# Retention queries and keys as block products, attention-value products in another order, bias rows made once

## The chip, the cores and the metric

The kernel runs on one core of one Trainium2 chip. The metric is the device time of one execution in microseconds (us), lower is better. The core has a matrix engine (PE; PEld is its weight loading), a vector engine (DVE), an activation engine (ACT), GpSimd (POOL) and a queue-only engine (SP), which run side by side and wait for one another through semaphores. Each engine works through its instructions in program order. SP, ACT and POOL issue DMAs; only POOL issues those that add to their destination.

## The reference, cut to what matters

Two layers (DEPTH 2) over 512 tokens of width 1024, float32. Each layer projects the input x to many columns at once and then mixes:

```python
z = einsum('bsd,dc->bsc', x, w_in) + b_in
q_a, k_a, v_a, q_r, k_r, v_r, g_r, gate_a, gate_b = split(z)
# attention: 18 heads of 64 in three groups (window, dilation)
# retention: 4 heads; q, k 256 wide, v and gate 512 wide
t1, t2 = t[..., :128], t[..., 128:]                 # rot(), for q and for k
rot = concatenate([t1 * cos - t2 * sin, t1 * sin + t2 * cos])
sc = (q . k) * decay_mask;  o = sc . v (+ state);   y_r = group_norm(o)
y_b = silu(g_r) * y_r
merged = sigmoid(gate_a) * (y_a @ w_attn_proj) + sigmoid(gate_b) * (y_b @ w_ret_proj)
x = layer_norm(ALPHA * x + merged @ w_out)
x = layer_norm(ALPHA * x + (silu(x @ w_gate) * (x @ w_up)) @ w_down)
```

What concerns the change is the first line: the columns of the attention values (v_a, 1152), of the retention queries and keys (q_r, k_r, 256 per head each) and of the retention values and gates (v_r, g_r, 512 per head each), with their biases, and the rotation of q_r and k_r.

## The kernel before

**Products.** Every float32 factor is split into a high part and a low part (`hilo`, L91: ACT casts the high part at L92, DVE subtracts it at L93), and every product is three matmuls of 128 rows (`mm3`, L80): high by high, high by low, low by high. All of them stand as L81 in the profile, since the helper `mm` holds the call. Weights come from memory into eight buffers (`raw`, 1024 float32 a partition) by SP, and their parts go into four buffers each of `whi` and `wlo`.

Three schemes make the projections:

- `wstat` (weights stationary, 512 tokens moving): 24 matmuls of 512 columns for 128 output columns. The queries and keys of all retention heads are made so: four `wstat`, 96 matmuls per head.
- `wide` (weights stationary, block scheme): two matrices of 256 output columns share seven block products instead of eight, on halves of the tokens and of the inner dimension. Each block product is 24 matmuls of 256 columns, 168 in all for 2 x 256 output columns. The merge gates and the FFN use it.
- `tall` (tokens stationary, weights moving): the same seven block products for 2 x n columns, each of 24 matmuls of n columns. The attention values use it (n = 288, two calls per layer, t = 0 and 1, called VA below), and the retention values and gates (n = 512, one call per head, called vg(0) to vg(3)).

The operands of the seven products come from class `Right`: four blocks B11, B21, B22 and (inside P1 and P3) B12 of the weights, and the sums P1 = B11 + B12, P3 = B12 + B22, P2 = P1 + B22, P4 = P2 + B21. P1 and P3 are made in memory traffic: SP loads one block (L109), and POOL issues a DMA that adds the other to it (L316). P2 and P4 are DVE additions in P1's buffer (L342). `operands` runs one product ahead: while PE works at one product, ACT (L325) and DVE (L331) make the parts of the next. For `tall` a product has two buffers (two units), for `wide` one.

The order of the products is a table. `ORDER`, which `tall` uses, is 1, 2, 5, 3, 6, 7, 4, with the operands B11, B21, P1, B22, P2, P3, P4. `WIDE` is 1, 5, 6, 2, 7, 3, 4, with the operands B11, P1, P2, B21, P3, B22, P4. Several products add up in one PSUM tile (`CHAIN`): 1, 6, 7, 4 in chain A, 5 and 3 in chain C, 2 alone. What has to leave the chain between two products is copied by ACT to a tile `sn` (L453), and DVE adds or subtracts (L460, L463).

**Order of the work.** The program is written by hand, engine by engine. One list, `side`, holds small pieces of other work (attention, scores and outputs of retention), and `tick` takes from it at the rate that `pace` sets, after each group of three matmuls. In `ret_outputs` of the head before, which runs beside `rotary(h)`, each of four pieces `one(i)` does matmuls (`px<-vr,pj`), statistics on DVE (L855 to L859), a power on POOL (L124) and three tiny DVE steps that wait for it (L125 to L127); `turn(i)` transposes the result.

**Around the change.** A layer begins with attention queries and keys, then VA for t = 0 and 1, then attention, then rotary(0) and vg(0), and for h = 1, 2, 3: rotary(h), vg(h). Each `tall` call is preceded by `bias_rows` (L429): POOL clears a `raw` buffer and loads the two biases into rows 0 and 32 by four small DMAs, DVE and ACT turn them into high and low parts in the one tile `bh`, and a matmul with `ones` as stationary operand (rows 0 and 32 are 1) puts the bias into PSUM. That is done 12 times, 4 for VA and 8 for the heads. In `rotary` (L645) DVE takes each of the four `wstat` results times cos and times sin, the bias added in the same step (L655), subtracts and adds (L659, L660), and `hilo` makes the parts, tile name `rot`.

The names in rows: `raw` a weight buffer, `whi` and `wlo` its parts, `xh`, `xl` the parts of the tokens, `xs` those of the sums of tokens, `ps` and `px` PSUM tiles, `rp` the rotated pieces, `rb` and `bh` the bias rows, `pj` the scores, `vr` the retention values.

Of the kernel before, what the change touches and what calls it, by code (L numbers as in the profile page):

```python
# [18 lines left out]
P = 128  # L19
# [34 lines left out]
def hybrid_kernel(ctx, tc, x, rel_bias, w_in, b_in, w_attn_proj, w_ret_proj, w_out,  # L54
# [40 lines left out]
    def raw(name="raw"):  # L95
        return rawp.tile([P, 1024], F32, tag="raw", name=name)
# [201 lines left out]
    WIDE = tuple(ORDER[i] for i in (0, 2, 4, 1, 5, 3, 6))  # L298
    WIDE1 = tuple(ORDER[i] for i in (0, 1, 2, 4, 3, 5, 6))
# [54 lines left out]
    def pair_right(w1, w2, c, order=WIDE):  # L354
# [17 lines left out]
    def tall(right, n, left, ev, bias_=None):  # L372


        ps = {}
        for (i, an, bn), units in zip(ORDER, right.operands()):
            ks = [(u, k) for u in units for k in range(u[0].shape[1])]
            c = CHAIN[i]
            for a in range(2):
                fresh = i in FIRST  # L380
                if fresh:
                    ps[c, a] = psum("ps")[:, :n]
                if bias_ is not None and i in (1, 5):
# [12 lines left out]
                if i == 6:  # L396
                    ev(3, a, ps["C", a])
            yield

    def wide(right, left, ev):  # L400
# [26 lines left out]

        return Right(src, [(k, n) for k in nk])

    def bias_rows(b1, b2):  # L430

        n = b1.shape[0]
        r = raw("rb")[:, :2 * n]
        pool.memset(r, 0.0)
        for q in (0, BK):
            pool.dma_start(r[q:q + 1, :n], b1.unsqueeze(0))
            pool.dma_start(r[q:q + 1, n:], b2.unsqueeze(0))
        dve.tensor_tensor(out=r[:, n:], in0=r[:, n:], in1=r[:, :n], op=ALU.add)
        h = bh[:, :2 * n]
        act.copy(out=h, in_=r)  # L440
        e = slice(BK, BK + 1)
        dve.tensor_tensor(out=h[e], in0=r[e], in1=h[e].bitcast(F32), op=ALU.subtract)
        return h

    def biased(right, n, rows_, left, right_done):
# [19 lines left out]
        return tall(right, n, x_left, ev, rows_)  # L465
# [158 lines left out]
    def layer(ly, cp):  # L624
# [16 lines left out]
        def slot(name="op", dt=F32R):  # L641
            return opp.tile([P, 2, S], dt, tag="op", name=name)

        def rotary(h):

            rot = []
            for c0 in (C_QR + h * RQ, C_KR + h * RQ):
                us = pair_units(w_l, c0)
                prod = []
                for t in range(2):  # L650
                    ps = wstat(us, t)
                    pr = []
                    for tb in (cos, sin):
                        m = work("rp")
                        dve.scalar_tensor_tensor(out=m, in0=ps, scalar=bcol(c0 + t * P), in1=tb, op0=ALU.add, op1=ALU.mult)  # L655
                        pr.append(m)
# [4 lines left out]
                pair = []
                for src in (t1c, t1s):
                    o_ = slot("rot")
                    hilo(src, o_[:, 0], o_[:, 1])
                    pair.append(o_)
                rot.append(pair)
            heads[h]["q"], heads[h]["k"] = rot

        def ret_values_gates(h):
            cv, cg = C_VR + h * RV, C_GR + h * RV  # L670
# [16 lines left out]
            rows_ = bias_rows(b_l[cv:cv + RV], b_l[cg:cg + RV])  # L687
            yield from biased(halves(w_l, 0, (2, 2), cv, cg, RV), RV, rows_, left, gate)

        with stage("attn") as ap_, stage("attw", 4) as aw:  # L690
            qk = {}
# [16 lines left out]
            if ly == 0:  # L708
# [28 lines left out]
                o32 = work("o32")
                dve.memset(o32[:, :P], 0.0)
                dve.memset(o32[0:1, :P], 1.0)
                dve.memset(o32[BK:BK + 1, :P], 1.0)  # L740
                act.copy(out=ones, in_=o32[:, :P])
# [16 lines left out]
            for t in range(2):  # L758
                c1, c2 = C_VA + t * VB, C_VA + (2 + t) * VB

                def put(i, s, c):
                    nc.sync.dma_start(v_d[i * P:(i + 1) * P, c - C_VA:c - C_VA + VB], s)

                def left(i, ps, s, c1=c1):
                    if s is None:
                        s = work("sn")[:, :VB]
                        act.copy(out=s, in_=ps)
                    else:
                        dve.tensor_tensor(out=s, in0=ps, in1=s, op=ALU.add)
                    put(i, s, c1)  # L770

                run(biased(halves(w_l, 0, (2, 2), c1, c2, VB), VB, bias_rows(b_l[c1:c1 + VB], b_l[c2:c2 + VB]),
                           left, lambda i, s, c2=c2: put(i, s, c2)))
            drain()

# [46 lines left out]
        with stage("ret") as rp:  # L822
            def ret_scores(h):
# [248 lines left out]
        def ffn_pair(f, o_):  # L1072
# [120 lines left out]
```

## Time and profile before

| what | value |
|---|---|
| median of 3 runs | 2190.7 us (2188.38 to 2191.09) |
| the profiled execution, its own time | 2188.09 us |
| its span, first to last instruction | 2186.3 us |
| granted PE clock, mean | 0.998 |
| busy share PE, PEld, DVE, ACT, POOL | 99%, 87%, 65%, 45%, 12% |

The span is 1.8 us shorter than the execution's own time, and the execution is 2.6 us under the median. The shares are averages over stages that differ: in the stretches of `rotary` DVE is nearer to full than the mean says, and PE, which is nearly always busy, has its few waits in some ten places.

### The profile page before, as it was taken

To read this page: it belongs to the slowest core of one execution; us is meant where nothing else is said; L and a number is where in the kernel's file an instruction comes from. 1 tells how busy PE (TensorE), PEld (TensorE's weight loads), DVE (VectorE), ACT (ScalarE), POOL (GpSimd) and SP (SyncE) were. 2 spreads that over 40 slices of the span, in tenths; PEclk is the share of its full clock that TensorE was granted. 3 is DMA by queue.
4 is the path that set the end of the run, shared out by engine and by line. 5 is a ranking of instruction groups with operands and counts; after the bars stand their busy time and mean duration, and the time that the engine had idled before them with its cause. 6 is when DMAs were issued, how large, how long until landed. Compare 5 with 4: busy or idle time off the path is not lost.

```text
span 2186.3 us, 32588 instructions
## 1 busy us (share of the span) xinstructions
PE 2160.0 (99%) x12906; PEld 1900.6 (87%) x12906; DVE 1412.5 (65%) x2035; ACT 988.1 (45%) x1597; POOL 254.1 (12%) x296
## 2 busy tenths in 40 slices
PE   8999999999999999999999999999999999999998
PEld 7977888889988899989898778888899889999996
DVE  5643677877655685747676446777777447766575
ACT  4444544545733263525245445445566233444350
POOL 3110011011000100000030100111110001000001
PEclk9999999999999999999999999999999999999999
DMA  8944266458685356656369342665577762666561
GB/s 228 244 125 104 58 165 159 132 136 192 192 307 189 91 150 133 172 134 156 95 158 260 90 92 74 152 180 144 137 191 223 267 194 58 172 150 165 123 163 39
DMA packets 305978, 338.60 MB, mean 155 GB/s; under 512 B 22862, under 2 KB 244194, under 8 KB 305697
## 3 DMA queue, kind: packets, MB, share of 16 engines
q1 hardware_dynamic: 227712, 248.81, 37.8%
q0 software_dynamic: 50832, 74.90, 18.2%
q10 hardware_dynamic: 27280, 12.80, 2.0%
q8 instruction: 101, 1.65, 0.3%
q14 instruction: 53, 0.43, 0.1%
HBM read 310.67 MB, written 28.53 MB: 155 GB/s over the span
## 4 chain that ended last, share of the span: by engine, by line
PE 82%; issue 9%; DMA 3%; DVE 3%; ACT 1%; POOL 1%; POOLq 0%; DVEq 0%; ACTq 0%; SPq 0%
PE ps L81 75%; PE px L81 5%; DMA raw<-in_w_in 2%; PE px L865 1%; PE px L533 1%; POOL ry L124 0%; DMA exd<-wb 0%; DVE wlo L331 0%; PE px L169 0%; DMA exd<-pk 0%; DVE wlo L93 0%; DVE xtok L988 0%; DMA mb<-exd 0%; DMA rb<-in_b_in 0%; ACT whi L92 0%
## 5 line engine op out<-in xcount | busy, mean ns | idle before, releaser
L331 DVE TENSOR_TENSOR wlo<-raw,whi 128x1024 fp32r<-128x1024 f32 (+1 forms) x364 | 418.1, 1150 | 210.0 <-ACT whi L325 207.3
L81 PE MATMUL ps<-xh,whi 128*128 128x256 f32 (+1 forms) x1536 | 515.7, 337 | 4.4 <-ACT whi L92 3.3
L325 ACT CAST whi<-raw 128x1024 fp32r<-128x1024 f32 (+1 forms) x364 | 358.8, 990 | 342.1 <-PE ps L81 198.5
L81 PE MATMUL ps<-xh,wlo 128*128 128x256 f32 (+1 forms) x1536 | 500.5, 327 | 1.1 <-DVE wlo L93 0.9
L81 PE MATMUL ps<-xl,whi 128*128 128x256 f32 (+1 forms) x1536 | 500.5, 326 | 0.2 <-DVE xl L93 0.2
L81 PE MATMUL ps<-xs,whi 128*128 128x256 f32 (+1 forms) x2048 | 404.6, 296 | 0.0
L81 PEld LDWEIGHTS ps<-xs,whi 128*128 128x128 f32 x2048 | 327.8, 191 | 10.3
L93 DVE TENSOR_TENSOR wlo<-raw,whi 128x1024 fp32r<-128x1024 f32 (+2 forms) x162 | 193.3, 1195 | 200.9 <-ACT whi L92 200.5
L81 PEld LDWEIGHTS ps<-xh,whi 128*128 128x128 f32 x1536 | 292.1, 191 | 33.6 <-issue 6.4
L81 PEld LDWEIGHTS ps<-xh,wlo 128*128 128x128 f32 x1536 | 292.5, 191 | 26.3 <-DVE wlo L93 1.5
L81 PEld LDWEIGHTS ps<-xl,whi 128*128 128x128 f32 x1536 | 293.5, 191 | 19.2 <-DVE xl L93 1.0
L81 PE MATMUL ps<-xs,wlo 128*128 128x256 f32 (+1 forms) x1024 | 303.4, 296 | 0.0
L92 ACT CAST whi<-raw 128x1024 fp32r<-128x1024 f32 (+2 forms) x162 | 165.2, 1028 | 235.1 <-PE ps L81 151.6
L81 PE MATMUL ps<-whi,xs 128*128 128x512 f32 (+1 forms) x768 | 219.9, 360 | 1.8 <-ACT whi L325 1.3
L81 PEld LDWEIGHTS ps<-xs,wlo 128*128 128x128 f32 x1024 | 196.0, 191 | 5.0
L81 PE MATMUL ps<-whi,ht 128*128 128x512 f32 x576 | 178.4, 389 | 0.0
L81 PEld LDWEIGHTS ps<-whi,xs 128*128 128x128 f32 x768 | 137.6, 188 | 22.5 <-ACT whi L325 1.8
L81 PE MATMUL ps<-wlo,xs 128*128 128x512 f32 (+1 forms) x384 | 138.1, 360 | 1.2 <-DVE wlo L331 1.2
L316 POOL DMA_DIRECT2D raw<-in_w_ffn_gate x40 | 51.7, 1293 | 680.3 <-DMA raw<-in_w_ffn_up 312.3
L81 PEld LDWEIGHTS ps<-whi,ht 128*128 128x128 f32 x576 | 108.1, 188 | 22.3
L316 POOL DMA_DIRECT2D raw<-in_w_in x64 | 80.3, 1273 | 358.2 <-DMA raw<-in_w_in 160.8
L342 DVE TENSOR_TENSOR raw<-raw 128x1024 f32<-128x1024 f32 (+1 forms) x104 | 119.5, 1149 | 2.1
(185 smaller groups left out, 2951.7 us busy)
## 6 DMA issues: line engine op xcount, KB each, us to landing
raw<-in_w_in SPq DMA_DIRECT2D x152, 512.0 KB, 4.2
raw<-in_w_ffn_up SPq DMA_DIRECT2D x64, 512.0 KB, 4.1
raw<-in_w_in POOLq DMA_DIRECT2D x48, 512.0 KB, 8.3
raw<-in_w_ffn_gate SPq DMA_DIRECT2D x44, 512.0 KB, 4.8
raw<-in_w_ffn_down SPq DMA_DIRECT2D x44, 512.0 KB, 4.1
raw<-in_w_ffn_gate POOLq DMA_DIRECT2D x40, 512.0 KB, 6.5
raw<-in_w_in SPq DMA_DIRECT2D x72, 256.0 KB, 5.3
raw<-in_w_ret_proj SPq DMA_DIRECT2D x32, 512.0 KB, 6.3
```

The costliest lines, as they stand in the source:

```text
L81: pe.matmul(ps, lhsT=a, rhs=b, start=start, stop=stop, skip_group_check=True)
L92: act.copy(out=hi, in_=src)
L93: dve.tensor_tensor(out=lo, in0=src, in1=hi.bitcast(F32), op=ALU.subtract)
L316: pool.dma_start(r, self.src({"P1": "B12", "P3": "B22"}[n], u), accum_op=ALU.add)
L325: act.copy(out=h, in_=src)
L331: dve.tensor_tensor(out=l, in0=src, in1=h.bitcast(F32), op=ALU.subtract)
L342: dve.tensor_tensor(out=r, in0=r, in1=self.t["B22" if n == "P2" else "B21", u], op=ALU.add)
L533: pe.transpose(px[:, (2 + j) * P:(3 + j) * P], s[:, hh, j * P:(j + 1) * P], ident)
L865: pe.transpose(px[:, t * P:(t + 1) * P], ys[i][:, t * P:(t + 1) * P], ident)
```

## The change

Five edits, of which the last is a renaming:

1. `bias_rows` runs once, in layer 0, for all 12 pairs of biases: one `raw` buffer, 16 small DMAs, one addition, one cast, one subtraction. The 12 pairs stand in rows 0 to 11 of `bh` (high) and 32 to 43 (low). The bias matmul's stationary operand is a column of a new tile `pick` (made from the identity matrix), broadcast over 128 columns; `ones` is gone.
2. `tall` takes the order from `Right`, whose default is now 1, 5, 6, 2, 7, 3, 4 (`SPACED`, the old `WIDE`), and loads B11, P3, P1, B22, B21 in that order. Product 3's result is no longer held back until product 6.
3. `rotary` for heads 1 to 3 makes queries and keys with `wide`: 168 matmuls of 256 columns. ACT copies the chain's first results with the bias added (`biased_copy`, two instructions each), DVE adds or subtracts the later products, and `turned` rotates each quarter (two multiplications of 512 elements, a subtraction and an addition of 256, then `hilo`). Head 0 keeps `wstat`. The tiles for queries and keys now hold high parts and low parts apart, and are taken at the start of `rotary`.
4. In layer 0 the copies of the first two token tiles (`xc`) on ACT go behind the parts of the first weights.
5. `WIDE` and `WIDE1` are named `SPACED` and `SUMS2`.

```diff
-        def __init__(self, src, shapes, order=ORDER, loads=("B11", "B21", "P1", "P3", "B22")):
+        def __init__(self, src, shapes, order=SPACED, loads=("B11", "P3", "P1", "B22", "B21")):
...
-        for (i, an, bn), units in zip(ORDER, right.operands()):
+        for (i, an, bn), units in zip(right.order, right.operands()):
...
-                    mm(ps[c, a], ones, bias_[:, (i != 1) * n:(i != 1) * n + n], True, False)
+                    o = (i != 1) * RV
+                    mm(ps[c, a], pick[:, bias_:bias_ + 1].to_broadcast([P, P]), bh[:, o:o + n], True, False)
...
-                if i != 3:
-                    ev(i, a, ps[c, a])
-                if i == 6:
-                    ev(3, a, ps["C", a])
+                ev(i, a, ps[c, a])
...
+        def turned(t, ts_, hi, lo):
+            n = t.shape[2]
+            s = view(work("rs"), 2, n)
+            cs, sn_ = (a[:, ts_].unsqueeze(1).to_broadcast([P, 2, n]) for a in (cos, sin))
+            dve.tensor_tensor(out=s, in0=t, in1=sn_, op=ALU.mult)
+            dve.tensor_tensor(out=t, in0=t, in1=cs, op=ALU.mult)
+            dve.tensor_tensor(out=t[:, 0], in0=t[:, 0], in1=s[:, 1], op=ALU.subtract)
+            dve.tensor_tensor(out=t[:, 1], in0=t[:, 1], in1=s[:, 0], op=ALU.add)
+            hilo(t, hi[:, :, ts_], lo[:, :, ts_])
...
+            def biased_copy(ps, c, sign=1.0):
+                o_ = view(work("sn"), 2, 256)
+                for q in range(2):
+                    act.activation(out=o_[:, q], in_=ps[:, q * 256:(q + 1) * 256], func=AF.Identity, bias=bcol(c + q * P), scale=sign)
+                return o_
+            def ev(i, ps):
+                p2 = ps.rearrange("p (q t) -> p q t", q=2)
+                if i in (1, 5):
+                    sn[i] = biased_copy(ps, cq if i == 1 else ck)
+                elif i == 6:
+                    sn[i] = biased_copy(ps, ck, -1.0)
+                elif i == 2:
+                    dve.tensor_tensor(out=sn[1], in0=p2, in1=sn[1], op=ALU.add)
+                    turned(sn[1], slice(0, 256), *heads[h]["q"])
...
+                elif i == 4:
+                    turned(biased_copy(ps, cq), slice(256, 512), *heads[h]["q"])
+            wide(pair_right(w_l[:, :, cq:], w_l[:, :, ck:], 0), x_left, ev)
```

In the program, 576 matmuls of 512 columns go and 1008 of 256 columns come, both over two layers of three heads.

The first place is DVE from the last quarter of rotary(2) to the first third of vg(2) in layer 0. Before, `rp` and `rot` are the pieces of the rotation, and the `wlo` rows prepare the next weights:

```order
404 L655 SCALAR_TENSOR_TENSOR rp<-ps,bT,cos 128x512
405 L655 SCALAR_TENSOR_TENSOR rp<-ps,bT,sin 128x512
406 L331 TENSOR_TENSOR wlo<-raw,whi 128x1024
407 L655 SCALAR_TENSOR_TENSOR rp<-ps,bT,cos 128x512
408 L655 SCALAR_TENSOR_TENSOR rp<-ps,bT,sin 128x512
409 L660 TENSOR_TENSOR rp<-rp 128x512
410 L659 TENSOR_TENSOR rp<-rp 128x512
411 L331 TENSOR_TENSOR wlo<-raw,whi 128x1024
412 L93 TENSOR_TENSOR rot<-rp,rot 128x512 x2
413 L331 TENSOR_TENSOR wlo<-raw,whi 128x1024
414 L342 TENSOR_TENSOR raw<-raw 128x1024
```

And in the changed program, from the addition of product 3 (L709) on (`sn` the quarter being rotated, `rs` its product with sin; the `wlo` row is for the second unit of B11 of vg(2)):

```order
409 L709 TENSOR_TENSOR sn<-ps,sn 128x512
410 L94 TENSOR_TENSOR rot<-sn,rot 128x2x256
411 L661 TENSOR_TENSOR sn<-sn,rs 128x256
412 L662 TENSOR_TENSOR sn<-sn,rs 128x256
413 L659 TENSOR_TENSOR rs<-sn,sin 128x512
414 L336 TENSOR_TENSOR wlo<-raw,whi 128x1024
415 L94 TENSOR_TENSOR rot<-sn,rot 128x2x256
416 L660 TENSOR_TENSOR sn<-sn,cos 128x512
417 L659 TENSOR_TENSOR rs<-sn,sin 128x512
418 L661 TENSOR_TENSOR sn<-sn,rs 128x256
419 L662 TENSOR_TENSOR sn<-sn,rs 128x256
420 L660 TENSOR_TENSOR sn<-sn,cos 128x512
```

The rows go on so, and two more `wlo` follow for the two units of P1:

```order
421 L336 TENSOR_TENSOR wlo<-raw,whi 128x1024
422 L94 TENSOR_TENSOR rot<-sn,rot 128x2x256
423 L661 TENSOR_TENSOR sn<-sn,rs 128x256
424 L662 TENSOR_TENSOR sn<-sn,rs 128x256
425 L336 TENSOR_TENSOR wlo<-raw,whi 128x1024
426 L94 TENSOR_TENSOR rot<-sn,rot 128x2x256
427 L347 TENSOR_TENSOR raw<-raw 128x1024 x2
```

Between the preparations of the weights stand four to six steps of the rotation where there were two to four, and the weights behind them are now those of P1.

The second place is POOL at the first VA of layer 0 (the `L316` and `L321` rows add to a weight buffer, `bias` is the attention's position bias). Before, the first two adding DMAs are those of P1 and the last two those of P3:

```order
30 L781 DMA bias_1420<-bias_r_84 128x128
31 L316 DMA raw_565<-in_w_in 128x2x288
32 L782 DMA bias_1420<-bias_r_84 128x128
33 L316 DMA raw_568<-in_w_in 128x2x288
34 L780 DMA bias_1424<-bias_r_84 128x256
35 L781 DMA bias_1424<-bias_r_84 128x128
36 L316 DMA raw_571<-in_w_in 128x2x288
37 L782 DMA bias_1424<-bias_r_84 128x128
38 L316 DMA raw_574<-in_w_in 128x2x288
```

And changed, the first two (569, 572) are P3's and the last two (575, 578) P1's:

```order
35 L321 DMA raw_569<-in_w_in 128x2x288
36 L827 DMA bias_1149<-bias_r_84 128x256
37 L321 DMA raw_572<-in_w_in 128x2x288
38 L828 DMA bias_1149<-bias_r_84 128x128
39 L829 DMA bias_1149<-bias_r_84 128x128
40 L827 DMA bias_1153<-bias_r_84 128x256
41 L828 DMA bias_1153<-bias_r_84 128x128
42 L321 DMA raw_575<-in_w_in 128x2x288
43 L829 DMA bias_1153<-bias_r_84 128x128
44 L827 DMA bias_1419<-bias_r_84 128x256
45 L321 DMA raw_578<-in_w_in 128x2x288
```

P1 has moved from the first two adding DMAs to the last two.

The third place is PE in the same VA, between its first product (B11) and the product of P1. Before, product 2 (B21) stands between them; here its last rows and P1's first, `xs` the token sums:

```order
295 L81 MATMUL ps<-whi,xh 128x288
296 L81 MATMUL ps<-wlo,xh 128x288
297 L81 MATMUL ps<-whi,xl 128x288
298 L81 MATMUL ps<-bh,ones 128x288
299 L81 MATMUL ps<-whi,xs 128x288
300 L81 MATMUL ps<-wlo,xs 128x288
```

Changed, the last rows of product 1 and then P1:

```order
269 L82 MATMUL ps<-whi,xh 128x288
270 L82 MATMUL ps<-wlo,xh 128x288
271 L82 MATMUL ps<-whi,xl 128x288
272 L82 MATMUL ps<-bh,pick 128x288
273 L82 MATMUL ps<-whi,xs 128x288
274 L82 MATMUL ps<-wlo,xs 128x288
```

P1's product comes 24 matmuls earlier on PE.

## Rows read from the trace of the kernel before

**Rows 1.** The page: busy time, share of the span, instructions

```profile
PE 2160.0 (99%) x12906; PEld 1900.6 (87%) x12906; DVE 1412.5 (65%) x2035; ACT 988.1 (45%) x1597; POOL 254.1 (12%) x296
```

**Rows 2.** Waits of PE: us in total, times, longest us

```profile
PE ps L81 <- ACT whi L92: 3.3, 1, 3.3
...
PE ps L81 <- DVE sn L460: 2.4, 4, 1.1
...
PE ps L81 <- ACT whi L325: 1.3, 2, 0.7
PE ps L81 <- DVE wlo L331: 1.2, 3, 0.4
...
PE ps L81 <- ACT sn L453: 0.3, 1, 0.3
```

**Rows 3.** Timeline of PE in rotary(2), layer 0: start us, us, instruction

```profile
437.08 0.39 PE L81 MATMUL ps<-xh,whi 128*128 128x512 f32 x1
...
438.21 0.39 PE L81 MATMUL ps<-xh,wlo 128*128 128x512 f32 x1
```

**Rows 4.** Busy by stretch (x instructions): rotary(2), vg(2), four FFN pairs; then clock, DMA

```profile
437.10:467.50 30.40, 30.40 (x143) 25.21 (x142) 21.09 (x44) 10.53 (x15) 7.21 (x8) 1.00 0.77 181
467.50:510.50 43.00, 43.00 (x198) 35.91 (x197) 34.38 (x42) 24.69 (x33) 3.87 (x3) 1.00 0.57 143
...
847.20:927.90 80.70, 80.70 (x674) 80.69 (x673) 57.47 (x61) 42.57 (x54) 5.12 (x4) 1.00 0.63 163
```

**Rows 5.** Timeline of DVE in rotary(2): start us, us, [idle before, releaser]

```profile
451.50 0.22 DVE L125 SCALAR_TENSOR_TENSOR rt<-ry,ve 128x1 f32<-128x1 f32 x1 [6.33 <-POOL ry L124]
...
453.08 0.69 DVE L855 BATCH_NORM_STATS2 st<-px 128x6 f32<-128x512 f32 x1
...
455.39 1.22 DVE L331 TENSOR_TENSOR wlo<-raw,whi 128x1024 fp32r<-128x1024 f32 x1
456.53 0.74 DVE L655 SCALAR_TENSOR_TENSOR rp<-ps,bT,cos 128x512 f32<-128x512 f32 x1
...
458.45 0.68 DVE L659 TENSOR_TENSOR rp<-rp 128x512 f32<-128x512 f32 x1
459.05 1.22 DVE L331 TENSOR_TENSOR wlo<-raw,whi 128x1024 fp32r<-128x1024 f32 x1
```

**Rows 6.** DVE by group and shape, whole run: xcount, busy us, mean ns

```profile
L523 DVE CUSTOM_DVE_ANT_0 s<-px,bias 128x256 f32<-128x256 f32 x84 | 32.4, 421 | 52.7 <-PE px L81 52.6
```

**Rows 7.** Timeline of POOL in rotary(2)

```profile
449.67 1.20 POOL L316 DMA_DIRECT2D raw<-in_w_in  x1 [4.12 <-DMA raw<-in_w_in]
450.42 1.04 POOL L124 TENSOR_TENSOR ry<-ve,mhalf 128x1 f32<-128x1 f32 x1
```

**Rows 8.** Timeline of PE in vg(0), layer 0

```profile
281.42 0.40 PE L81 MATMUL ps<-whi,xs 128*128 128x512 f32 x1
282.87 0.47 PE L81 MATMUL ps<-whi,xh 128*128 128x512 f32 x1 [1.06 <-DVE sn L460]
```

**Rows 9.** Timeline of PE at the start of VA, t = 0, layer 0

```profile
52.95 0.29 PE L81 MATMUL ps<-bh,ones 128*128 128x288 f32 x1
53.08 0.29 PE L81 MATMUL ps<-whi,xh 128*128 128x288 f32 x1
```

**Rows 10.** Timeline of POOL before and in that VA

```profile
48.19 1.26 POOL L316 DMA_DIRECT2D raw<-in_w_in  x1 [1.36 <-DMA raw<-in_w_in]
...
49.52 1.75 POOL L316 DMA_DIRECT2D raw<-in_w_in  x1
...
52.20 1.51 POOL L316 DMA_DIRECT2D raw<-in_w_in  x1
...
55.80 1.21 POOL L316 DMA_DIRECT2D raw<-in_w_in  x1 [1.50 <-DMA raw<-in_w_in]
```

**Rows 11.** DMA issues from 41 to 60 us: engine, count, KB each, median us to landing

```profile
raw<-in_w_in POOLq DMA_DIRECT2D x4, 288.0 KB, 7.3
```

**Rows 12.** Timeline of ACT in that VA: the last part of P1 made

```profile
58.08 0.67 ACT L325 CAST whi<-raw 128x576 fp32r<-128x576 f32 x1 [1.08 <-DMA raw<-in_w_in]
```

More of the change, by code (lines that the diff above doesn't have):

```diff
@@ L69, in hybrid_kernel @@
     mhalf = keep.tile([P, 1], F32, name="mhalf")
-    ones = keep.tile([P, P], F32R, name="ones")
+    NR = DEPTH * (RH + 2)
+    pick = keep.tile([P, NR], F32R, name="pick")
     bh = keep.tile([P, 1024], F32R, name="bh")
@@ L156, in hybrid_kernel, with to_xT @@
     STEP = 0.68
-    def to_xT(src, i, cp):
+    def to_xT(src, i, cp, late=None):
         awaited[i] = 2
@@ L173, in one @@
             if cp is not None:
-                act.copy(out=cp[i // 2][hf][:, :, (i % 2) * P:(i % 2 + 1) * P], in_=pv)
+                o_ = cp[i // 2][hf][:, :, (i % 2) * P:(i % 2 + 1) * P]
+                if late is None:
+                    act.copy(out=o_, in_=pv)
+                else:
+                    late.append(lambda: act.copy(out=o_, in_=pv))
         return [lambda hf=hf: one(hf) for hf in range(2)]
@@ L428, in halves, with va_row, bias_rows, biased @@
         return Right(src, [(k, n) for k in nk])
-    def bias_rows(b1, b2):
-        n = b1.shape[0]
-        r = raw("rb")[:, :2 * n]
+    def va_row(ly, t):
+        return DEPTH * RH + 2 * ly + t
+    def bias_rows():
+        r = raw("rb")
         pool.memset(r, 0.0)
         for q in (0, BK):
[L436 to L445, printed above, removed]
+            for ly in range(DEPTH):
+                for b2 in range(2):
+                    o, e = b2 * RV, (C_VR, C_GR)[b2]
+                    pool.dma_start(r[q + ly * RH:q + (ly + 1) * RH, o:o + RV],
+                                   b_in[ly, e:e + RH * RV].rearrange("(h n) -> h n", h=RH))
+                    e = C_VA + 2 * b2 * VB
+                    pool.dma_start(r[q + va_row(ly, 0):q + va_row(ly, 2), o:o + VB],
+                                   b_in[ly, e:e + 2 * VB].rearrange("(h n) -> h n", h=2))
+        dve.tensor_tensor(out=r[:, RV:], in0=r[:, RV:], in1=r[:, :RV], op=ALU.add)
+        act.copy(out=bh, in_=r)
+        e = slice(BK, 2 * BK)
+        dve.tensor_tensor(out=bh[e], in0=r[e], in1=bh[e].bitcast(F32), op=ALU.subtract)
+    def biased(right, n, row, left, right_done):
         sn = {}
@@ L463, in ev @@
                 left(2 + a, ps, None)
-        return tall(right, n, x_left, ev, rows_)
+        return tall(right, n, x_left, ev, row)
     bias_d = drp.tile([HPG, L0 + 2 * L1], F32, name="bias_d")
@@ new lines, in rotary @@
+        def rotary(h):
+            cq, ck = C_QR + h * RQ, C_KR + h * RQ
+            for n_ in "qk":
+                heads[h][n_] = [slot("rot") for _ in range(2)]
+            if h == 0:
+                for c0, n_ in ((cq, "q"), (ck, "k")):
+                    us = pair_units(w_l, c0)
+                    prod = []
+                    for t in range(2):
+                        ps = wstat(us, t)
+                        pr = []
+                        for tb in (cos, sin):
+                            m = work("rp")
+                            dve.scalar_tensor_tensor(out=m, in0=ps, scalar=bcol(c0 + t * P), in1=tb, op0=ALU.add, op1=ALU.mult)
+                            pr.append(m)
+                        prod.append(pr)
+                    (t1c, t1s), (t2c, t2s) = prod
+                    dve.tensor_tensor(out=t1c, in0=t1c, in1=t2s, op=ALU.subtract)
+                    dve.tensor_tensor(out=t1s, in0=t1s, in1=t2c, op=ALU.add)
+                    for t, src in enumerate((t1c, t1s)):
+                        hilo(src, heads[h][n_][0][:, t], heads[h][n_][1][:, t])
+                return
+            sn = {}
+            def biased_copy(ps, c, sign=1.0):
[12 more added lines that the diff above has]
+                    turned(sn[1], slice(0, 256), *heads[h]["q"])
+                elif i == 7:
+                    dve.tensor_tensor(out=sn[5], in0=sn[5], in1=p2, op=ALU.subtract)
+                    turned(sn[5], slice(256, 512), *heads[h]["k"])
+                elif i == 3:
+                    dve.tensor_tensor(out=sn[6], in0=p2, in1=sn[6], op=ALU.add)
+                    turned(sn[6], slice(0, 256), *heads[h]["k"])
+                elif i == 4:
+                    turned(biased_copy(ps, cq), slice(256, 512), *heads[h]["q"])
+            wide(pair_right(w_l[:, :, cq:], w_l[:, :, ck:], 0), x_left, ev)
@@ L729, in layer @@
                 cp = x_copies()
-                ops = [to_xT(x0[i].rearrange("p a b -> p (a b)"), i, cp) for i in range(NI)]
+                late = []
+                ops = [to_xT(x0[i].rearrange("p a b -> p (a b)"), i, cp, late if i < 2 else None) for i in range(NI)]
                 for f in ops[0] + ops[1]:
@@ L733, in layer @@
                 make()
+                for f in late:
+                    f()
                 us0 = [first, qk_units(0, 1)]
@@ L736, in layer @@
                 side.extend([lambda l_=l_: bias_cols(l_) for l_ in range(DEPTH)] + vecs[:3] + ops[2] + vecs[3:] + ops[3])
[L737 to L741, printed above, removed]
+                dve.tensor_tensor(out=pick, in0=ident[:, :NR], in1=ident[:, BK:BK + NR], op=ALU.add)
                 rate[0], credit[0] = 0.4, 0.0
@@ L770, in left @@
                     put(i, s, c1)
[L772 removed]
+                run(biased(halves(w_l, 0, (2, 2), c1, c2, VB), VB, va_row(ly, t),
                            left, lambda i, s, c2=c2: put(i, s, c2)))
```

41 lines of the change are left out of this document (10 added, 31 removed).

## The prediction

> **What bounds the kernel now.** I began with the busy shares: PE is busy 2160.0 of 2186.3 us [rows 1]. Only two things can therefore shorten the run, fewer PE microseconds of work or the few waits; and whatever makes PE wait lengthens it one for one. Then the list of PE's waits [rows 2]: the entries that the change touches are the parts of weights that ACT and DVE make (3.3 us on L92, once, at the start; 1.3 and 1.2 us on L325 and L331) and the results that must leave a PSUM chain (2.4 us on L460, 0.3 on L453). Then the stretches: in rotary(2) DVE is busy 21.09 of 30.40 us and DMA 0.77, in vg(2) 34.38 of 43.00 [rows 4]. So the rotations are where PE's work is cut, and DVE is the engine to watch there.
>
> **The change, part by part.**
>
> *Rotations of heads 1 to 3.* The 512-column matmuls start 0.226 us apart (438.21 - 437.08 over five steps [rows 3]), 96 of them 21.7 us. The 256-column ones of the same scheme as the new rotary start 80.70 / 674 = 0.120 us apart with DVE at 0.71 and DMA at 0.63 [rows 4], 168 of them 20.1 us. That is 1.6 us less in each of six rotations (three heads, two layers), **-9.6 us**; side pieces are the same number, each with the same small restart.
>
> *What that asks of DVE.* From starts in a row: a 1024-wide subtraction is followed 1.14 us later (455.39 to 456.53), a 512-wide one 0.60 later (458.45 to 459.05) [rows 5], each about 0.08 less than its duration; a 256-wide one lasts 0.42 [rows 6], so by the same cut 0.33. A block rotation needs 7 low parts and 2 sums of weights, 9 x 1.14 = 10.3; three additions of products, 1.8; four quarters of 3 x 0.60 + 2 x 0.33 = 2.46, 9.8: 21.9 us. The four output pieces of the head before take about 2.3 each (453.08 to 455.39 [rows 5]), 9.2. Together 31.1 us, where PE will take 30.4 - 1.6 = 28.8. Before, it was 4 low parts, 8 fused products of 0.66, 8 steps of 0.60, so 14.7 + 9.2 = 23.9 in 30.4. DVE thus becomes the fuller engine in these stretches. It may run behind, since vg has slack (34.38 of 43.00), but only until PE asks for what DVE has not made. That is at the start of vg, in DVE's order (the first place above): from the subtraction of product 7 (L706, row 402) to the low part of P1's second unit (row 425) there are 12 steps of 0.60, 8 of 0.33, 3 of 1.14 and a tiny one, 13.4 us. PE in the same time does products 3 and 4 (48 x 0.120 = 5.8), about 0.6 of transposes, product 1 of vg (26 x 0.227 = 5.9) and 8 matmuls of P1 (1.8), 14.1 us. DVE arrives at row 402 some 0.7 to 1.5 late, because in PE's product 7 (2.9 + 0.6 us) it has 4.2 us to do (two low-part-sized or yb steps, two halves of the rotation, the fourth output piece with its power on POOL). So PE waits 0 to 0.8 us. There are new waits too: `rs` of the third quarter reuses a work buffer that a y_d store must leave, and behind it on DVE stands the low part of vg's second unit. I take 0.8 us a head, **+4.8 us**; bounds 0 and 3.0 (the latter if each step costs its whole duration, 1.22, 0.68 and 0.42: 15.3 instead of 13.4, and 0.3 more ahead of it).
>
> [...]
>
> *POOL's power.* The 6.33 us that DVE waited at 451.50 [rows 5] came from a power queued behind an adding DMA (449.67, itself 4.12 after its load [rows 7]). In the changed order two powers stand ahead of vg's last two adding DMAs instead of one, and the loads before them can start earlier, when product 5 and 6 are at work. I expect this wait to shrink to 1 us or less. It costs nothing now and its end gives nothing by itself, but it is why DVE can do 31 us of work at all.
>
> *The order of `tall`: chains.* With 1, 5, 6, 2 a chain is no longer asked for again right after its last matmul: product 2 (its own tile) stands between 6 and 7, and 3 between 7 and 4. The waits on L460 and L453 are 2.4 + 0.3 us [rows 2], in vg(0) of both layers, three each; each restart costs some 0.15 more than the idle shown (281.42 to 282.87 is 1.45, 1.22 over a step, where 1.06 is idle [rows 8]): **-3.6 us**, bounds -3.6 and 0 (if the same evictions are late elsewhere).
>
> *The order of `tall`: P1 earlier.* P1's product starts one product after the first instead of two. In VA of layer 0, t = 0, that is 52.95 + 26 x 0.133 = 56.4 us [rows 9]; its second unit is wanted 0.9 us later. P1's adding DMAs were the first two on POOL, issued at 48.19 and 49.52 after their loads, landing 7.3 us later in the median [rows 10, 11]; the second landed so that ACT's part was made at 58.08 to 58.75 [rows 12], with nobody waiting. Now they are the last two, after P3's. If they land as before (their loads keep their places in SP's queue, fifth and sixth), PE waits 58.75 - 57.3 = 1.5 plus 0.6 for the low part, 2 us. If they take the places of the old last two (52.20 and 55.80 [rows 10]), 55.80 + 7.3 + 1.4 = 64.5, PE waits 7 us. I take **+3.0**, nearer to the first, since P3's loads now land early and its adding DMAs are then out of the way. In t = 1 of both layers the present waits (1.3 + 1.2 us of rows 2 are mostly these) are of the same kind; P1 is wanted 3.2 us earlier, but one buffer fewer is taken by bias rows; with layer 1's t = 0: **+0.7**, bounds -3 and +6. In vg(1) to vg(3) P1's loads are some 14 us early, nothing.
>
> *Bias rows once.* Eleven memsets, casts and 32 small DMAs go, none of which PE waits for: 0. If the one run, behind the position tables on POOL's early idle time, were late, PE's bias matmul at 52.95 has 35 us in hand. A broadcast stationary operand is not in this trace; its weight load is one of 0.19 us if it costs what the others do: 0, at most 48 x 0.19 = 9 us if none of them is hidden, which the nearest row, the `ones` matmul of 0.13 us spacing [rows 9], speaks against.
>
> *Copies later in layer 0.* The first weights' parts come sooner by up to four copies; the 3.3 us wait [rows 2] is for the first of them, which mostly waits for data. I take **-0.3**, bounds -1.9 and +0.5.
>
> Sum: -9.6 + 4.8 - 3.6 + 3.0 + 0.7 - 0.3 = -5.0. The profiled execution took 2188.1 us (span 2186.3 and 1.8 around it) and is 2.6 under the median, 2190.7. So 2183.1 for a like execution, **2185.7** for the median.
>
> **Rivals.**
> - *DVE hides it all (faster).* PE waits for nothing at the start of vg, and VA waits 1.5 us less: -5.0 - 4.8 - 1.5 = -11.3, 2179. For it: DVE no longer loses 6.33 us to POOL. Against it: 31.1 us of work in 28.8.
> - *DVE takes the gain (no change).* PE waits 1.6 us at the start of each of six vg: -5.0 + 4.8 = -0.2, 2190.5. For it: the small margin of 14.1 against 13.4. It decides if DVE reaches row 402 over 2.3 us late.
> - *DVE is the bound and the kernel is slower.* Each step on DVE costs its whole duration, 3.0 us a head: -5.0 + 13.2 = +8.2, 2199. It decides from 2.0 us a head up (the gain of 9.6, 3.6 and 0.3 less 3.7 in VA is spent at 1.6). [...] Against it: the starts in rows 5.
> - *P1 late in every VA.* The four VA wait 7, 3, 3 and 3 us: -5.0 + 12.3 - 3.7 + 3 (the old waits stay) = +3 to +6, 2194 to 2197. For it: POOL's queue, where 12 position-bias DMAs are mixed among the four. Against it: P3's loads are earlier now.
>
> **How the numbers follow.** What a measurement of this kernel can tell from no change is about 0.2%, 4.4 us: faster is under 2186.3, slower over 2195.1. The forecast has 0.50 (own range 2181 to 2190; 0.28 of it faster, 0.22 the same), DVE hiding it all 0.18 (faster), DVE taking the gain 0.14 (0.02 faster, 0.10 same, 0.02 slower), DVE the bound 0.10 (slower), P1 late 0.08 (0.03 same, 0.05 slower). That makes 0.48, 0.35 and 0.17. The range reaches from the first rival, a little beyond it, to where the third begins to lie outside: 2176 to 2198.
>
> **What would show it.** Rotations of heads 1 to 3 at 0.120 us a matmul and some 28.8 us long; DVE with hardly an idle microsecond in them; PE waits on L336 (`wlo`, the line after the change) in the first 9 us of vg(1) to vg(3), 0 to 1 us each; no waits on the results of `sn` in vg(0); waits on `whi` and `wlo` at 57 us and around the second VA of both layers, 2 to 4 us the first. I am wrong if the waits at the start of vg are over 1.5 us a head, if the first VA waits over 5 us, or if a bias matmul with the broadcast operand shows a step over 0.2 us.

## The result, and the profile after

The changed kernel takes 2197.5 us in the median of 9 runs (2194.1 to 2199.4); before took 2190.7 beside it. The ratio is 1.0028, 95% interval 1.0019 to 1.0038: **slower by 0.28%**, some 6 us. I had forecast 2185.7, faster. The time lies just inside my range of 2176 to 2198, but the sign is wrong. That it lies inside is luck: the upper end came from the rival in which DVE is the bound, and that is not what happened.

The busy shares and PE's waits of the changed kernel, in the form of [rows 1, 2] (a line number is a few higher: L330 and L336 make the weights' high and low parts):

```profile
PE 2161.4 (99%) x13338; PEld 1923.5 (88%) x13338; DVE 1435.4 (65%) x2083; ACT 1018.0 (46%) x1651; POOL 243.4 (11%) x265
...
PE ps L82 <- ACT whi L330: 7.7, 5, 2.6
PE ps L82 <- ACT whi L93: 3.0, 2, 1.7
PE px L599 <- DVE y L594: 2.4, 2, 1.3
...
PE ps L82 <- DVE wlo L336: 1.9, 6, 0.4
```

The waits on chain results (L460, L453) are gone, and two new ones have come: 7.7 us on high parts of weights, and 2.4 us on attention's last outputs, which now come due in vg(0) where the chain results did.

Now the stretches, in the columns of [rows 4]: rotary(2), vg(2), and then VA of layer 0 and of layer 1:

```profile
444.50:473.20 28.70, 28.70 (x216) 27.45 (x214) 23.74 (x50) 15.64 (x24) 5.83 (x7) 1.00 0.82 189
473.20:516.20 43.00, 43.00 (x199) 35.87 (x197) 37.08 (x47) 25.69 (x36) 3.89 (x3) 1.00 0.64 158
...
53.20:112.00 58.80, 52.08 (x345) 50.06 (x344) 32.34 (x49) 24.98 (x44) 9.75 (x12) 0.91 0.79 205
1140.90:1193.60 52.70, 49.63 (x345) 48.59 (x345) 32.36 (x49) 24.61 (x44) 4.79 (x4) 0.94 0.73 191
```

The same two VA before:

```profile
52.95:101.10 48.15, 46.73 (x345) 45.96 (x344) 32.45 (x50) 25.11 (x44) 10.07 (x12) 1.00 0.94 237
1135.10:1182.50 47.40, 46.35 (x345) 45.88 (x344) 32.55 (x50) 25.09 (x44) 8.67 (x10) 1.00 0.88 216
```

The rotation took 28.70 us instead of 30.40, and vg(2) 43.0 as before, with PE busy in every microsecond: the gain that I forecast came in full. VA lost it: 58.80 instead of 48.15 and 52.70 instead of 47.40, with the same 345 matmuls, **15.9 us**. PE's idle time there rose from 48.15 - 46.73 = 1.4 to 6.7 us and from 1.1 to 3.1, 7.3 together; for the rest PE is busy longer for the same work: a matmul behind a wait lasts 0.40 us instead of 0.29 (below), and the mean granted clock is 0.91 and 0.94, where it was 1.00.

How that looks at the second call in layer 0: PE (first fence), then ACT, which makes P1's high parts (second), then the stretch behind the waits (third).

```profile
85.78 0.30 PE L82 MATMUL ps<-bh,pick 128*128 128x288 f32 x1
88.32 0.40 PE L82 MATMUL ps<-whi,xs 128*128 128x288 f32 x1 [2.24 <-ACT whi L330]
89.11 0.40 PE L82 MATMUL ps<-wlo,xs 128*128 128x288 f32 x1 [0.39 <-DVE wlo L336]
...
92.73 0.44 PE L82 MATMUL ps<-bh,pick 128*128 128x288 f32 x1
92.97 0.44 PE L82 MATMUL ps<-whi,xs 128*128 128x288 f32 x1
```

```profile
87.59 0.67 ACT L330 CAST whi<-raw 128x576 fp32r<-128x576 f32 x1 [6.28 <-DMA raw<-in_w_in]
89.85 0.67 ACT L330 CAST whi<-raw 128x576 fp32r<-128x576 f32 x1 [1.29 <-DVE raw L347]
```

```profile
89.40:96.22 6.82, 6.52 (x26) 5.85 (x26) 5.57 (x8) 3.72 (x8) 0.00 (x0) 0.50 0.40 132
```

P1's product begins at 85.78 with its bias and then waits until P1's first adding DMA has landed at 87.5 (issued at 78.53). The second, issued at 79.90, landed at 89.8, just before the cast at 89.85; the row names a sum on DVE that ended at the same moment. The step from matmul to matmul at 92.73 is 0.24 us where [rows 9] have 0.13, and the granted clock of this stretch is 0.50. From 83 to 88 us it was 1.00, from 88 to 93 its mean is 0.64, from 93 to 100 0.77, and from 100 to 112 it is 1.00 again.

### The profile page after: what moved, and what is told of

The parts are those of the page before. It is cut to its first block, busy times and chain, and to the rows that moved or that the text cites. A ratio compares the mean times of both kernels' runs of the same rounds, so it can differ in the third digit from the quotient of the medians.

```text
span 2192.8 us, 33542 instructions
## 1 busy us (share of the span) xinstructions
PE 2161.4 (99%) x13338; PEld 1923.5 (88%) x13338; DVE 1435.4 (65%) x2083; ACT 1018.0 (46%) x1651; POOL 243.4 (11%) x265
## 4 chain that ended last, share of the span: by engine, by line
PE 88%; DMA 4%; issue 4%; DVE 2%; ACT 1%; POOL 1%; SPq 0%; POOLq 0%; ACTq 0%; DVEq 0%
PE ps L82 79%; PE px L82 7%; DMA raw<-in_w_in 2%; PE px L543 1%; DMA exd<-wb 1%; PE px L912 1%; POOL ry L125 0%; PE px L170 0%; DMA exd<-pk 0%; DMA mb<-exd 0%; DVE wlo L336 0%; DVE xtok L1035 0%; ACT whi L330 0%; DMA raw<-in_w_ffn_gate 0%; DMA v_d<-sn 0%
## 5 line engine op out<-in xcount | busy, mean ns | idle before, releaser
L336 DVE TENSOR_TENSOR wlo<-raw,whi 128x1024 fp32r<-128x1024 f32 (+1 forms) x406 | 467.9, 1157 | 253.0 <-ACT whi L330 252.0
L330 ACT CAST whi<-raw 128x1024 fp32r<-128x1024 f32 (+1 forms) x406 | 402.5, 996 | 386.2 <-PE ps L82 201.7
L82 PE MATMUL ps<-xh,whi 128*128 128x256 f32 (+1 forms) x1488 | 479.9, 324 | 4.1 <-ACT whi L93 3.0
L82 PE MATMUL ps<-xs,whi 128*128 128x256 f32 (+1 forms) x2432 | 476.8, 295 | 0.0
L82 PE MATMUL ps<-xh,wlo 128*128 128x256 f32 (+1 forms) x1488 | 466.5, 315 | 1.0 <-DVE wlo L94 1.0
L82 PE MATMUL ps<-xl,whi 128*128 128x256 f32 (+1 forms) x1488 | 467.0, 315 | 0.2 <-DVE xl L94 0.2
L82 PEld LDWEIGHTS ps<-xs,whi 128*128 128x128 f32 x2432 | 388.1, 191 | 11.3
L82 PE MATMUL ps<-xs,wlo 128*128 128x256 f32 (+1 forms) x1216 | 357.6, 294 | 0.0
L94 DVE TENSOR_TENSOR wlo<-raw,whi 128x1024 fp32r<-128x1024 f32 (+2 forms) x138 | 164.0, 1191 | 190.0 <-ACT whi L93 188.4
L93 ACT CAST whi<-raw 128x1024 fp32r<-128x1024 f32 (+2 forms) x138 | 140.8, 1024 | 236.4 <-PE ps L82 142.7
L82 PEld LDWEIGHTS ps<-xs,wlo 128*128 128x128 f32 x1216 | 232.7, 191 | 5.0
L82 PEld LDWEIGHTS ps<-whi,xs 128*128 128x128 f32 x768 | 143.1, 195 | 28.9 <-ACT whi L330 9.4
L321 POOL DMA_DIRECT2D raw<-in_w_in x76 | 96.0, 1264 | 644.6 <-DMA raw<-in_w_in 195.1
L321 POOL DMA_DIRECT2D raw<-in_w_ffn_gate x40 | 51.8, 1295 | 680.9 <-DMA raw<-in_w_ffn_up 327.1
```

The lines of the kernel that those rows point to most:

```text
L82: pe.matmul(ps, lhsT=a, rhs=b, start=start, stop=stop, skip_group_check=True)
L93: act.copy(out=hi, in_=src)
L94: dve.tensor_tensor(out=lo, in0=src, in1=hi.bitcast(F32), op=ALU.subtract)
L321: pool.dma_start(r, self.src({"P1": "B12", "P3": "B22"}[n], u), accum_op=ALU.add)
L330: act.copy(out=h, in_=src)
L336: dve.tensor_tensor(out=l, in0=src, in1=h.bitcast(F32), op=ALU.subtract)
```

## The experiments

I began with theory Q: in VA, P1 is wanted one product earlier while its adding DMAs have become the last on POOL. Its rivals: P1 too early wherever it stands (W), and the bias rows made once (B).

**VA alone put back (e1_va_old).** The edit passes the old order and loads to the two VA calls of a layer; its other lines let `halves` hand them on and hold product 3's result back until product 6 again:

```diff
-                run(biased(halves(w_l, 0, (2, 2), c1, c2, VB), VB, va_row(ly, t),
+                run(biased(halves(w_l, 0, (2, 2), c1, c2, VB, ORDER, ("B11", "B21", "P1", "P3", "B22")), VB, va_row(ly, t),
...
```

> The changed kernel with the two attention-value calls (VA) of each layer put back to the old order 1, 2, 5, 3, 6, 7, 4 and the old loads; all else as changed. Theory Q (the loss is P1 wanted one product earlier while its adding DMAs come last on POOL): the PE waits of 4.9, 4.4 and 4.4 us and the lower clock behind them go, VA takes about 48.2 us in layer 0 and 47.4 in layer 1 as before, and the kernel takes some 16 us less than the changed one, about 2181.5. Rival B (the loss is in the bias rows made once, the broadcast operand, or the buffers and traffic that they shift): VA stays over 52 us in layer 0, and the time over 2190.

Measured: 2177.1 us, ratio to before 0.9941 (0.9925 to 0.9956). VA of both layers:

```profile
52.58:99.32 46.74, 46.59 (x346) 45.94 (x344) 31.49 (x48) 24.56 (x43) 8.35 (x9) 1.00 0.89 219
1128.41:1176.08 47.67, 46.60 (x346) 45.95 (x345) 31.31 (x48) 24.35 (x43) 4.75 (x4) 1.00 0.80 200
```

They are 1.4 us shorter and 0.3 us longer than before, at full clock. The loss is the new order in VA with its loads, not bias rows made once. This version is faster than both kernels, by 0.59% and by some 19 us.

**P1's loads first, the new order kept (e2_p1_first).**

```diff
-                run(biased(halves(w_l, 0, (2, 2), c1, c2, VB), VB, va_row(ly, t),
+                run(biased(halves(w_l, 0, (2, 2), c1, c2, VB, SPACED, ("B11", "P1", "P3", "B22", "B21")), VB, va_row(ly, t),
...
```

> The changed kernel with one tuple changed, for VA alone: the loads are B11, P1, P3, B22, B21, so P1's adding DMAs are POOL's first two and P3's the last two, while the products keep the new order. Theory Q: P1's sums land as early as P3's do now (52.7 and 55.5 us in the first VA, 81.8 and 84.7 in the second), PE waits under 1 us in each VA, the clock stays, about 2181 to 2184. Rival W (P1 is wanted too early wherever it stands in the queue, since its loads wait for buffers): two of the four VA still wait over 2 us, 2188 or more.

Measured: 2179.0 us, 0.9946 (0.9932 to 0.9961). PE waits in VA of layer 0, all of them:

```profile
PE ps L82 <- DVE wlo L336: 2.1, 1, 2.1
```

Two names in a tuple are worth 18 us. Q's time came out (2179 where it said 2181 to 2184). Two of the single waits are longer than Q said, this one of 2.1 us and one of 1.5 in layer 1, but they are not P1's, so they do not speak for W. P1's product ran from 80.75 to 84.22 without a wait; the wait stands in the next one, P2's. DVE, then PE:

```profile
85.90 0.76 DVE L347 TENSOR_TENSOR raw<-raw 128x576 f32<-128x576 f32 x1 [1.71 <-DMA raw<-in_w_in]
86.58 0.75 DVE L336 TENSOR_TENSOR wlo<-raw,whi 128x576 fp32r<-128x576 f32 x1
...
87.39 0.40 PE L82 MATMUL ps<-wlo,xs 128*128 128x288 f32 x1 [2.07 <-DVE wlo L336]
```

The low part of P2's second unit (86.58) stands on DVE's queue behind the sum for P4 (85.90), which waits for a unit of B21, now the last load (landed at 85.8). Both VA take 48.2 us here, against 48.15 and 47.40 before. So the order of products does nearly no harm in VA if the order of loads follows it.

**The new order alone, in the kernel before (e3_order_only).** `tall` takes the new order and loads; nothing else is changed.

> The kernel before with only the new order of products and loads in every tokens-stationary call (VA and vg); rotations and bias rows as before. Theory Q: VA loses here as in the changed kernel, 10 us in layer 0 and 5 in layer 1, the waits on chain results in vg(0) go (1 to 3 us back), so 2202 to 2206. Rival B: the order alone does no harm without the bias rows made once, within 3 us of 2190.7.

Measured: 2205.4 us, 1.0068 (1.0054 to 1.0083). VA of layer 0 and 1:

```profile
53.18:113.85 60.67, 53.01 (x345) 50.78 (x344) 33.61 (x51) 25.47 (x45) 10.25 (x15) 0.89 0.76 202
1146.36:1205.47 59.11, 51.05 (x346) 48.91 (x345) 33.34 (x51) 25.33 (x45) 7.43 (x9) 0.91 0.71 186
```

As Q said: the order loses by itself, here 12 us in each layer. In layer 1 it loses more than with the bias rows made once (59.1 against 52.7), which was the first sign that these are not worth nothing.

**VA and vg put back (e4_tall_old).** As the first, and the same arguments for `halves` in `ret_values_gates`.

> The changed kernel with the old order in VA and in vg, so the rotations as block products, the bias rows made once and the later copies are what is left of the change. Theory Q: the rotations' 1.8 us each stay (six, 10.8 us), bias rows cost nothing, vg(0)'s waits on chain results come back: 2181 to 2184, and 0 to 2 us above the kernel with VA alone put back. Rival (DVE is what the order relieves at the start of vg(1) to vg(3)): PE waits of a microsecond or more there, 2188 or more.

Measured: 2195.2 us, 1.0023 (1.0010 to 1.0035). Here the rival was right: with the block rotations, vg needs the new order. rotary(1), vg(1), rotary(2), vg(2):

```profile
288.40:318.90 30.50, 28.82 (x214) 27.34 (x213) 20.72 (x45) 14.19 (x22) 7.76 (x9) 1.00 0.74 178
318.90:364.90 46.00, 43.72 (x199) 35.86 (x198) 40.13 (x54) 28.13 (x40) 3.21 (x3) 1.00 0.59 157
364.90:396.90 32.00, 29.02 (x216) 27.53 (x214) 21.10 (x45) 13.38 (x21) 7.14 (x8) 1.00 0.72 163
396.90:442.70 45.80, 45.12 (x198) 36.77 (x197) 39.95 (x53) 27.93 (x39) 3.19 (x3) 0.96 0.59 157
```

46 where it was 43, and 32 where it was 28.7. (The profiled execution took 2202.3 us, the longest of twelve, so these stretches show more than the median's loss.) DVE and POOL in rotary(2) say why:

```profile
394.01 0.22 DVE L126 SCALAR_TENSOR_TENSOR rt<-ry,ve 128x1 f32<-128x1 f32 x1 [5.96 <-POOL ry L125]
```

```profile
392.18 1.19 POOL L321 DMA_DIRECT2D raw<-in_w_in  x1 [8.78 <-DMA raw<-in_w_in]
392.94 1.04 POOL L125 TENSOR_TENSOR ry<-ve,mhalf 128x1 f32<-128x1 f32 x1
```

It is the wait of [rows 5, 7] again: the power stands behind an adding DMA, which waits for its load, which waited for a weight buffer (SP issued it at 382.97, when DVE had made the low part of 381.72 to 382.95, and it landed at 391.6). Before, the wait cost nothing; here DVE has the block rotations behind it on its queue, and they come 6 us late.

**The power taken off POOL (e6_pow_dve).** To tell that wait from plain lack of DVE time, in the kernel of the experiment before, DVE multiplies where POOL raised to a power; the retention outputs get another scale.

```diff
...
-        pool.tensor_tensor(out=y, in0=ve, in1=mhalf, op=ALU.pow)
+        if ret:
+            dve.tensor_tensor(out=y, in0=ve, in1=mhalf, op=ALU.mult)
+        else:
+            pool.tensor_tensor(out=y, in0=ve, in1=mhalf, op=ALU.pow)
...
```

> The kernel with the old order in VA and vg (e4_tall_old), with the power in the retention outputs left out: DVE multiplies in its place, so the retention outputs are scaled by another factor, and DVE no longer waits for POOL there. Theory P (in e4 vg(1) to vg(3) lose 3 to 6 us each because the power stands on POOL behind vg's last adding DMA, and DVE waits 6 us for it): the DVE waits on POOL go, vg is 42.7 to 43.5 us again, the time is 2177 to 2180. Rival D (DVE has too much to do in the rotations, with or without that wait): vg stays over 44.5 us, 2188 or more.

Measured: 2174.3 us, 0.9928 (0.9915 to 0.9940), and rotary(2) and vg(2):

```profile
360.30:389.00 28.70, 28.70 (x216) 27.45 (x214) 23.79 (x53) 15.17 (x23) 4.77 (x4) 1.00 0.76 177
389.00:432.00 43.00, 43.00 (x198) 35.90 (x197) 37.20 (x48) 26.27 (x37) 3.16 (x3) 1.00 0.66 170
```

With that wait gone the old order costs nothing in vg(2), nor in the other heads. DVE had time enough (23.8 of 28.7 us); it lost its time waiting. This is not a kernel to keep, since its output is another.

**The waits in VA filled with work (e5_fill).** The changed kernel, with 18 matmuls that nobody reads put into the gaps of the three VA calls that wait:

```diff
+                if i == 5 and a == 0 and bias_ in (8, 9, 11):
+                    px = psum()
+                    for _ in range(18):
+                        mm(px[:, :n], xh[:, 0, :P], xh[:, 1, :n], True, True)
```

> The changed kernel with 18 matmuls of 288 columns put ahead of P1's product in the three VA that wait (2.4 us each, into a PSUM tile that nobody reads). Theory K (part of the loss is the clock: after each wait the granted clock stood at 0.64 to 0.87 for 6 to 12 us): the waits are filled, the clock stays near 1.0 in VA, and the time falls by about 4 us, to 2193 or 2194, though work was added. Rival (the clock's fall costs nothing, or comes from elsewhere): the same time as the changed kernel or up to 2 us more, and VA as long as before the edit.

Measured: 2191.1 us, 1.0006 (0.9997 to 1.0015), against the changed kernel's 1.0028 a gain of 0.22%, 4.8 us, with 7.2 us of matmuls added. VA:

```profile
53.40:109.30 55.90, 52.35 (x380) 50.73 (x379) 32.00 (x49) 24.50 (x44) 9.94 (x12) 1.00 0.80 208
1141.00:1191.80 50.80, 49.19 (x364) 48.29 (x363) 32.03 (x49) 24.53 (x44) 4.79 (x4) 1.00 0.75 195
```

2.9 and 1.9 us shorter, at a clock of 1.00. So holding the clock gives back 4.8 of the 15.9 us, as theory K said, and about 11 are the waits themselves. A count agrees: of VA's matmuls 57 start 0.20 to 0.26 us after the one ahead of them in the changed kernel and 4 before, where the others take 0.13; that is 5.6 us.

**Bias rows per call, VA put back (e7_bias_each).** The first experiment with the old `bias_rows` and `ones`.

> The kernel with the old order in VA alone (e1_va_old), with the bias rows made before each call as before the change. My prediction's term (bias rows made once are worth nothing): 2176 to 2179, as e1. Rival (they take a weight buffer and a place on POOL's queue where loads are late): the second VA of each layer waits 1 to 2 us again, 2179 to 2183.

Measured: 2194.1 us, 1.0022 (1.0013 to 1.0031): 17 us above the first experiment, far more than the rival gave. VA of layer 0, and rotary(1):

```profile
54.65:106.87 52.22, 48.98 (x346) 47.53 (x345) 32.50 (x50) 24.90 (x44) 10.26 (x12) 0.97 0.90 229
295.40:329.50 34.10, 30.75 (x214) 28.94 (x215) 28.48 (x59) 18.31 (x29) 7.79 (x9) 0.95 0.83 195
```

And POOL and DVE just ahead of that rotary(1):

```profile
282.03 1.29 POOL L321 DMA_DIRECT2D raw<-in_w_in  x1 [8.80 <-DMA raw<-in_w_in]
...
284.58 0.55 POOL L441 DMA_DIRECT2D rb<-in_b_in  x1 [0.30 <-POOL rb L439]
...
292.28 0.69 DVE L443 TENSOR_TENSOR rb<-rb 128x512 f32<-128x512 f32 x1 [6.34 <-DMA rb<-in_b_in]
...
296.75 1.21 DVE L336 TENSOR_TENSOR wlo<-raw,whi 128x1024 fp32r<-128x1024 f32 x1
298.21 1.22 DVE L336 TENSOR_TENSOR wlo<-raw,whi 128x1024 fp32r<-128x1024 f32 x1
```

DVE waits 6.3 us with the bias rows of vg(1) in hand and the low parts that rotary(1) needs at 295.4 behind it. The four small DMAs of the bias rows, of 2 KB each, were issued from 284.58 to 286.12 and landed from 291.6 to 292.2, just behind the adding DMA that POOL had issued at 282.03 and that landed at 291.5. This rotary(1) takes 5.4 of the 17 us. VA of layer 0 ends 7.6 us later than in the first experiment, ahead of every rotation, and rotary(1) and vg(1) of layer 1 lose 5 together; heads 2 and 3 lose nothing (28.7 us a rotation). What cost the time in these other places was not traced.

**Rotations undone, VA put back (e8_rot_undone).** The first experiment with `wstat` for all four heads.

> The kernel with the old order in VA alone (e1_va_old), with the queries and keys of heads 1 to 3 made as before (96 matmuls of 512 columns per head). Theory: the six rotations take 30.4 instead of 28.7 us and nothing else moves, so 10 to 11 us above e1, 2187 to 2189: the rotations are worth their matmuls in full, and the rest of the change (bias rows once, the order in vg, the later copies) is worth some 2 us. Rival (DVE's fuller queue costs PE something elsewhere in e1, which goes here): less than 6 us above e1.

Measured: 2187.2 us, 0.9995 (0.9986 to 1.0004): 10.1 us above the first experiment by the medians, 11.8 by the two ratios. rotary(1) took 30.5 us again, vg(1) 43.0:

```profile
288.50:319.00 30.50, 30.50 (x143) 25.21 (x142) 22.02 (x45) 10.86 (x16) 5.36 (x7) 1.00 0.67 173
319.00:362.00 43.00, 43.00 (x197) 35.86 (x196) 32.32 (x41) 25.04 (x33) 3.03 (x3) 1.00 0.47 124
```

The rotations are worth their matmuls in full, once DVE is not held up. Without them, what is left of the change with the old order in VA cannot be told from no change.

## Why the prediction was wrong

The step that failed is "The order of `tall`: P1 earlier": +3.7 us forecast for the four VA, 15.9 measured. Three things were wrong in it.

- I called P3's loads "out of the way". They are ahead: P1's two sums now landed 8.2 and 4.9 us after their issue at 50.45 and 55.99, so ACT's two casts came at 58.79 and 60.96, and PE, at P1's bias matmul at 56.66, waited until 59.51. POOL, ACT and PE:

```profile
50.45 2.34 POOL L321 DMA_DIRECT2D raw<-in_w_in  x1
55.99 1.24 POOL L321 DMA_DIRECT2D raw<-in_w_in  x1 [1.44 <-issue]
...
58.79 0.67 ACT L330 CAST whi<-raw 128x576 fp32r<-128x576 f32 x1 [8.63 <-DMA raw<-in_w_in]
60.96 0.67 ACT L330 CAST whi<-raw 128x576 fp32r<-128x576 f32 x1 [1.50 <-DMA raw<-in_w_in]
...
56.66 0.29 PE L82 MATMUL ps<-bh,pick 128*128 128x288 f32 x1
59.51 0.40 PE L82 MATMUL ps<-whi,xs 128*128 128x288 f32 x1 [2.55 <-ACT whi L330]
```

  The call took 29.1 us (53.21 to 82.32) where it had taken 23.0 (52.95 to 75.97): 6.1 us more, near my upper end of 7 and not near the 3.0 that I took.
- For the other calls I took +0.7, because P1 had waits there already. I should have applied the same reckoning to them: P1 two places later on POOL and 3.2 us earlier on PE. The second calls of both layers lost some 5 us each; the first of layer 1 lost nothing. Of my rival "P1 late in every VA" this is the mechanism and, in three of four calls, the place, and its 2194 to 2197 was nearest to the result. I gave it 0.08. Its sum was wrong besides: 12.3 is already 16 less the 3.7, which is then taken off again, and 3 is added for old waits that the kernel before has too. Put right it is -5.0 + 12.3 = +7.3, 2198, or some 2195.5 if the old 2.5 us are part of the 16.
- I had no price for the clock, though it cost 4.8 us.

None of my three signs of being wrong came up: PE waits for nothing at the start of vg(1) to vg(3), the first VA waits 3.8 us, the bias matmul has a step of 0.13. I had set none for the second calls.

The other steps:

- *Rotations*, -9.6: right. Measured from the stretches, 6 x 1.7 = 10.2, and 10 to 12 by undoing them.
- *DVE*, +4.8: too much. The steps on DVE start 0.60, 0.33 and 1.14 us apart, as I took from [rows 5, 6], though each lasts longer:

```profile
468.50 0.69 DVE L659 TENSOR_TENSOR rs<-sn,sin 128x512 f32<-128x512 f32 x1
469.10 0.42 DVE L661 TENSOR_TENSOR sn<-sn,rs 128x256 f32<-128x256 f32 x1
469.43 0.42 DVE L662 TENSOR_TENSOR sn<-sn,rs 128x256 f32<-128x256 f32 x1
...
472.84 1.22 DVE L336 TENSOR_TENSOR wlo<-raw,whi 128x1024 fp32r<-128x1024 f32 x1
473.98 0.68 DVE L94 TENSOR_TENSOR rot<-sn,rot 128x512 fp32r<-128x512 f32 x1
```

  vg(1) to vg(3) wait for nothing (43.0 us, PE busy throughout). The rival in which each step costs its whole duration fell with it. What I named as the reason that DVE can do so much work held: in the six rotations DVE waits 0.2 us for POOL's powers, where it waited 37 before. I gave this no worth by itself; the fourth experiment shows that without it the rotations' gain is lost, 18 us between the versions with the new and the old order in vg.
- *Chains*, -3.6: the waits on L460 and L453 went, but 2.4 us on attention's outputs (L594) came up in the same place, and vg(0) gained some 1.3 us in both layers together. The bound "late elsewhere" was the better one.
- *Bias rows once*, 0: wrong in the changed program, where they are worth 17 us with the old order in VA. The one part that is traced is rotary(1) of layer 0, where they stand on DVE's queue ahead of weights that are due. Even with the rotations as before they were not quite free: in the last experiment VA takes 46.15 and 45.83 us where it took 48.15 and 47.40, and PE no longer waits in it (the copies in layer 0 differ there too).

```profile
1133.71:1179.54 45.83, 45.83 (x345) 45.83 (x344) 31.67 (x48) 24.86 (x43) 4.78 (x4) 1.00 0.85 206
```

- *Broadcast operand*: 0.13 us a step, as the `ones` matmul. Right.
- *Copies in layer 0*: the wait on the first high parts is 3.0 in two pieces instead of 3.3 in one; VA began at 53.2 instead of 52.95. Nothing, as good as forecast.

Put together: -10.2 (rotations) + 15.9 (VA) - 1.3 (vg(0)) = +4.4, of the 6.5 us between the two spans; the other 2 us lie in the attention stretches (143.1 and 144.4 us, before 142.7 and 142.9), which differ by about as much between runs of other versions. I did not trace them; in layer 1 the granted clock is 0.50 from 1294.3 to 1297.7 us.

## What to carry to other kernels

When an order of work is changed, follow every operand that moves forward back through the queue that makes it, and move its place in that queue as well: here two names in a tuple of loads were worth 18 us. Judge the parts of a change together: what is hidden before (here a power behind a DMA) is paid for as soon as another part gives the engine that hid it work that somebody waits for. And price a wait of PE with what the clock does after it: here 4.8 us beside some 11 of waits.

## What I had not expected of the hardware

The clock fell although PE was not idle for long at a stretch: 2.24 us and then short waits between single matmuls at 88 to 92 us, with the clock at 0.64 from 88 to 93, 0.77 until 100 and 1.00 after. Filled with matmuls that nobody reads, the same stretch stayed at 1.00. A single wait of 2.07 us with no others close behind it, in the second experiment, left it at 1.00 as well (the mean from 53.0 to 101.1 us).
